# Prompt projections of q, k and the two z: three 256-column matmuls per step, or one of 512 and one of 256

## The chip, the cores and the metric

The kernel runs on one core of a Trainium2 chip. The metric is device time in microseconds of one execution: the median of three runs. One further execution was profiled; views of that profile are quoted below. Engines go by the profile's names: PE (matmul), PEld (weight load of PE), DVE, ACT, POOL (elementwise engines), SP (issues most DMAs).

## The reference

One encoder layer is applied to two inputs, a prompt of 256 tokens and a sample of 2048, each with 1024 features:

```python
def encoder_layer(x, w_in, rpb, w_fourier, b_fourier, g_pre, g_na, g_f, w_out, g_post):
    h = rms_norm(x, g_pre)
    proj = h @ w_in
    q, k, v, z_a, u_f, z_f = jnp.split(proj, ...)   # 512 columns each
    y_a = neighbourhood_attention(q, k, v, rpb)
    y_f = fourier_mix(u_f, w_fourier, b_fourier)
    mixed = jnp.concatenate([rms_norm(y_a, g_na) * jax.nn.silu(z_a),
                             rms_norm(y_f, g_f) * jax.nn.silu(z_f)], axis=-1)
    out = mixed @ w_out
    return x + rms_norm(out, g_post)
```

The change concerns four of the six projections of the prompt: z_f, z_a, k and q, with silu taken of the two z at once.

## The kernel before

Everything is float32. A product is made of three matmuls in the rounded type fp32r: each operand is split into a high part (a rounded copy, made by ACT) and a low part (the operand less its high part, made by DVE), and high x high, low x high and high x low are added up in PSUM. `mm3` issues these three (lines 164 to 166).

The kernel first projects v and u of the prompt and of part of the sample (to 72 us in the profile). Then comes the loop that is changed: 16 blocks, `for b in range(16)`, with `kind, blk = divmod(b, 4)`: blocks 0 to 3 are z_f, 4 to 7 z_a, 8 to 11 k, 12 to 15 q. A block holds 128 output features for all 256 prompt tokens; it sums over 8 steps k of 128 input features. Weights are the stationary side; the tokens (`ph`, `pl` in the profile, made once ahead of the loop from `xp`) are the moving side, 256 columns. So a block is 8 x 3 matmuls of 256 columns into one PSUM tile `mm`. PSUM tiles `mm` rotate over five buffers. After block b, ACT empties it into a tile `f` (three buffers) with Silu for blocks 0 to 7 and as a plain copy for 8 to 15 (line 806); for z_f and k the copy also reorders the tokens. SP stores `f` to memory (lines 808 and 810).

Other work is written out between the blocks, in program order on each engine:

- `wz_load` in blocks 1 to 9: SP loads raw weights `wr`, four or more blocks before they are split.
- `b_raw(b + 2)` in blocks 2 to 13: ACT makes `wh` (below: wh(b + 2)), DVE makes `wl` (wl(b + 2)), lines 575 to 579. So the weights of a block are split two blocks ahead of it.
- `n_scale` in blocks 2 to 7: two DVE scalings of sample tokens, `nx` (line 413).
- `n_sum` in blocks 8 to 11: one DVE sum or difference of 2048 elements each (line 436).
- `n_first` in blocks 5, 12 and 14: ACT makes `xh`, DVE `xl` of sample tokens (lines 441 and 442).
- `op_split` in blocks 14 and 15: ACT and DVE make `vh` and `vl`, the first two of the weights that the next stage uses (lines 490 and 491).

The next stage, `vu`, projects sample tokens in groups of 12 matmuls of 512 columns; its groups j = 0, 1, 2 ... come two at a time and use the split weights `vh`, `vl` of number j. The weights for j = 2 and 3 are loaded by SP (line 476) behind the store of block 15. ACT empties the groups of j = 0 (line 521).

Nothing runs on POOL during the loop. In later stages it subtracts and adds elementwise, among them 128x512 sums of raw weights (line 545) beside DVE's splits of weights (line 560).

Of the kernel before, what the change touches and what calls it, by code (L numbers as in the profile page):

```python
# [11 lines left out]
F32R = mybir.dt.float32r  # L12
AF = mybir.ActivationFunctionType
ALU = mybir.AluOpType
# [3 lines left out]
TP, TS = 256, 2048  # L18
T = TP + TS
D = 1024  # L20
KC = 8
# [141 lines left out]
def mm3(nc, out, lh, ll, rh, rl, first, last):  # L163
    nc.tensor.matmul(out, lh, rh, start=first, stop=False)  # L164
    nc.tensor.matmul(out, lh, rl, start=False, stop=False)  # L165
    nc.tensor.matmul(out, ll, rh, start=False, stop=last)  # L166
# [8 lines left out]
def build(tc, A, O):  # L175
    nc = tc.nc
# [48 lines left out]
    def mmt(n):  # L225
        x = mmc[0] % 5 > 2
        mmc[0] += 1
        return ps.tile([128, n], F32, tag="t" if x else "a", name="mm", bufs=2 if x else 3)
# [24 lines left out]
    def k8(dtype, name, shape=(128, 4, 512)):  # L253
        return hp.tile(list(shape), dtype, tag="k8", name=name, bufs=NK)
# [35 lines left out]
    def x_split(c, ks=slice(0, 8), vec=False):  # L290
        if c not in xh:
            xh[c] = gt(BS, F32R, "xh"), gt(BS, F32R, "xl")
        h, l = xh[c][0][:, ks], xh[c][1][:, ks]
        src = x_first(c, ks.start // 2) if c < 3 else xs[c][:, ks]
        (nc.vector.tensor_copy if vec else nc.scalar.copy)(h, src)
        nc.vector.tensor_tensor(out=l, in0=src, in1=h.bitcast(F32), op=ALU.subtract)
# [24 lines left out]
    def iv_rows(c0, n):  # L321
        ivr[c0] = ps.tile([128, 128], F32, tag="c", name="ivt", bufs=1)[:n]
        nc.tensor.transpose(ivr[c0], invt[:, c0:c0 + n], ident)
# [6 lines left out]
    def iv_get(c0, n):  # L330
        t = ivb[c0] = st.tile([128, 512], F32, tag="e", name="iv", bufs=6) if n == 2 else \
            hp.tile([128, 1024], F32, tag="vw", name="iv", bufs=3)
        nc.sync.dma_start(t[:, :128 * n],
                          ivD[c0:c0 + n].rearrange("(o c) p -> o (c p)", o=1).to_broadcast([128, 128 * n]))

    def p_mm(m, c, kps, kks=None):
        if (m, c) not in acc:
            acc[m, c] = ps.tile([128, 512], F32, tag="b", name="mm", bufs=2) if (m, c) == ("u", 2) else mmt(512)
        xh_, xl_ = xh[c]
        for kk in kks or range(2 * kps[0], 2 * kps[-1] + 2):  # L340
            (mm3 if kk > 1 or m == "u" else mm3x)(nc, acc[m, c], xh_[:, kk], xl_[:, kk], W[m][kk][0], W[m][kk][1],
                                                  kk == 0, kk == KC - 1)

    def vu_out(m, c):
        s, b = PL[c]
        o = st.tile([128, 512], F32, tag="f", name=m + "o", bufs=3)
        x = row_tile(c)
        nc.scalar.activation(o, acc.pop((m, c)), AF.Copy, scale=invt[:, x:x + 1])
        if s is not None:
            put_rows(m, 0, b, s, o)  # L350
        elif m == "u":
            nc.sync.dma_start(uD[c * 128:c * 128 + 128, :], o)
        else:
            for r in range(4):
                nc.sync.dma_start(vP[c, r, 8 * c:8 * c + 32], o[32 * r:32 * r + 32])
                x = 24 * (1 - c)
                nc.sync.dma_start(vP[1 - c, r, 32 * c:32 * c + 8], o[32 * r + x:32 * r + x + 8])
# [38 lines left out]
    f_ = lambda t: t.bitcast(F32)  # L396

    def n_load(x):
        if type(x) is tuple:
            nq[x] = k8(F32, "nx")  # L400
            nc.sync.dma_start(nq[x], A["xq"][0, x[0], x[1]])
            return
        nx = [k8(F32, "nx") for kh in range(2)]
        for kh in range(2):
            for b in range(2):
                nq[x, kh, b] = nx[kh][:, 2 * b:2 * b + 2]
                nc.sync.dma_start(nq[x, kh, b], A["xq"][1, kh, b][:, 2 * x:2 * x + 2])
# [57 lines left out]
    def r_put(x):  # L465
        nc.sync.dma_start(sD[x], (RU[1], RV[0], RU[0], RU[1], RV[1])[x])
# [26 lines left out]
    def et(name):  # L493
        return st.tile([128, 512], F32, tag="e", name=name, bufs=6)
# [76 lines left out]
    def b_raw(b):  # L571
        wh, wl = [gt(BS, F32R, "w" + x) for x in "hl"]
        src = wp_[b]
        if b < 12:
            nc.scalar.copy(wh, src)
            nc.vector.tensor_tensor(out=wl, in0=src, in1=wh.bitcast(F32), op=ALU.subtract)
        else:
            nc.scalar.activation(wh, src, AF.Copy, scale=-0.125)
            nc.vector.scalar_tensor_tensor(out=wl, in0=src, scalar=-0.125, in1=wh.bitcast(F32), op0=ALU.mult,
                                           op1=ALU.subtract)  # L580
        wb[b] = wh, wl
# [46 lines left out]
    def x_first(c, kp):  # L628
        return x0[kp][:, 8 * (kp == 0):][:, :768].rearrange("p (c k t) -> p c k t", c=3, t=128)[:, c]
# [79 lines left out]
    def wz_load(n):  # L709
        for x in range(n):  # L710
            wp_.append(load(BS, A["wz"][len(wp_)], "wr"))
# [17 lines left out]
    for c in range(3, 6):  # L729
        if c == 3:  # L730
            iv_get(0, 2)
        if c < 5:
            wz_load(3)
            x_split(c + 1)
        if c == 3:
            r_put(1)
        if c == 4:
            n_load((0, 0))
            iv_get(2, 8)
            r_put(2)  # L740
            xp = k8(F32, "xp", (128, KC, 256))
            hp_, lp_ = [k8(F32R, "p" + x, (128, KC, 256)) for x in "hl"]
            for k in range(KC):
                for t in range(2):
                    ts = slice(128 * t, 128 * t + 128)
                    nc.vector.scalar_tensor_tensor(out=xp[:, k, ts], in0=x_first(t, k // 2)[:, k % 2], scalar=gpre[:, k:k + 1],
                                                   in1=ivb[0][:, ts], op0=ALU.mult, op1=ALU.mult)
            nc.scalar.copy(hp_, xp)
            nc.vector.tensor_tensor(out=lp_, in0=xp, in1=f_(hp_), op=ALU.subtract)
        if c == 5:  # L750
            n_load((1, 0))
            b_raw(0)
            b_raw(1)
        p_mm("v", c, range(4))
        vu_out("v", c)
        if c == 5:
            b_raw(2)
            b_raw(3)
            wz_load(1)
            n_load((0, 1))  # L760
            n_scale(None, 0, 0)
            n_first(0)
        p_mm("u", c, range(4))
        if c == 3:
            iv_rows(2, 8)
        vu_out("u", c)
        if c == 3:
            iv_put(2, 8)


    for b in range(16):
        kind, blk = divmod(b, 4)
        if 1 <= b < 10:
            wz_load(1)
        if b == 2:
            n_load((1, 1))
        if b in (5, 7):
            r_put(b // 2 + 1)
        if b == 10:
            op_load(0)  # L780
        if b == 12:
            op_load(1)
        if 2 <= b < 14:
            b_raw(b + 2)
        if 2 <= b < 8:
            x, y = divmod(b, 2)
            n_scale(None, *divmod(x, 2)[::-1], range(2 * y, 2 * y + 2))
        elif 8 <= b < 12:
            n_sum(b - 8)
        if b in (5, 12):  # L790
            n_first((5, 12).index(b) + 1)
        if b > 13:
            op_split(b - 14)
        if b == 14:
            n_first(3)
        p = mmt(512)[:, :TP]
        wh, wl = wb.pop(b)
        for k in range(KC):
            mm3(nc, p, wh[:, k], wl[:, k], hp_[:, k], lp_[:, k], k == 0, k == KC - 1)
        o = st.tile([128, 256], F32, tag="f", name="f", bufs=3)  # L800
        if kind % 2:
            i, d = p, o
        else:
            i = p.rearrange("p (b r c) -> p b r c", b=2, c=32)
            d = o.rearrange("p (r b c) -> p b r c", b=2, c=32)
        nc.scalar.activation(d, i, AF.Silu if kind < 2 else AF.Copy)
        if kind < 2:
            nc.sync.dma_start(zD[kind, blk * 128:blk * 128 + 128, :TP], o)
        else:
            nc.sync.dma_start((kD if kind == 2 else qD)[blk, :, :TP], o)  # L810
# [42 lines left out]
    for i in range(16):  # L853
# [14 lines left out]
        kind, blk = divmod(2 * pair(i), 4)  # L868
        o = [st.tile([128, 1024], F32, tag="f", name="f", bufs=3) for x in range(2)]
# [31 lines left out]
        for j in range(7):  # L901
            for f, d in ((u_load, 0), (u_split, 4), (u_stage1, 6)):
                x = 7 * pr + j - 7 - d
# [33 lines left out]
            if sg == 0:  # L937
                x, y = divmod(7 * (pr - 1) + j, 14)
# [29 lines left out]
            p = mmt(512)  # L968
# [673 lines left out]
    for k in range(2, len(G) + 1):  # L1642
        pr, i = divmod(k, 9)
# [17 lines left out]
        if k in WK:  # L1661
            y = WK.index(k)
            nc.sync.dma_start(WO[y % 2][:, y // 2].bitcast(F32), woD[y % 2, y // 2])
        x = k // 2 + 1
# [65 lines left out]
        if 32 <= k < 36:  # L1730
            x, d = k - 32, atiles[k - 32]
# [120 lines left out]
```

## Time and profile before

| what | us |
|---|---|
| median of 3 runs (lowest to highest) | 958.73 (958.66 to 958.79) |
| span of the profiled execution, first to last instruction | 957.4 |
| PE busy in it | 949.5 |
| DVE, ACT, POOL busy in it | 707.8, 494.8, 435.4 |
| the 16 blocks, first matmul to the next stage's first | 72.00 to 118.28 |

For the profiled execution no time besides its span is given; the span lies 1.3 us below the median of the runs. In the rows of the profile a line holds start and duration in us, or a count, a total and a mean; "x2" at a row's end says that two instructions were merged, and their joint stretch is given. Instructions on one engine start up to 0.1 us before the row ahead of them ends, since an engine takes up the next while it finishes the last. A matmul's duration includes its way through the array; the distance between two starts is what it costs. "out<-in" are the program's names for tiles.

### The profile page before, as it was taken

How to read it: one execution, taken by the hardware profiler on the slowest of the kernel's cores; microseconds unless marked ns; L12 is line 12 of the kernel's file. 1: busy time of each engine (PE TensorE's matmuls, PEld its weight loads, DVE VectorE, ACT ScalarE, POOL GpSimd, SP SyncE). 2: the span in 40 equal slices, each digit the busy share in tenths (PEclk: the TensorE clock that was granted, in tenths of full speed). 3: DMA queues.
4: the chain of work that ended last, by engine and by line, in shares of the span. 5: the costliest groups of instructions: out<-in, count | busy, mean ns of one | idle time of the engine just before them, and what ended most of it. 6: DMA issues, size and time to landing. Idle time of an engine off the chain costs nothing.

```text
span 957.4 us, 16751 instructions
## 1 busy us (share of the span) xinstructions
PE 949.5 (99%) x5625; PEld 790.3 (83%) x5625; DVE 707.8 (74%) x1298; ACT 494.8 (52%) x1068; POOL 435.4 (45%) x411
## 2 busy tenths in 40 slices
PE   9999999999999999999999999999999999999997
PEld 8889988888888888888888779788788888888886
DVE  6758987787975865697887369776666656659997
ACT  6735676423334532233344267677676766644443
POOL 4100002465750302575566055567678686524444
PEclk9999999999999999999999999999999999999998
DMA  9899697557758894499889997788877998989993
GB/s 357 297 383 334 245 343 264 187 193 280 296 190 331 304 342 144 175 345 356 306 297 340 335 329 247 232 241 271 262 241 239 285 301 255 287 289 346 330 346 129
DMA packets 140077, 269.80 MB, mean 282 GB/s; under 512 B 13178, under 2 KB 80464, under 8 KB 136728
## 3 DMA queue, kind: packets, MB, share of 16 engines
q1 hardware_dynamic: 139640, 268.32, 80.5%
q8 instruction: 45, 0.74, 0.3%
q10 hardware_dynamic: 288, 0.40, 0.1%
q14 instruction: 40, 0.33, 0.1%
q0 software_dynamic: 64, 0.02, 0.0%
HBM read 179.00 MB, written 96.81 MB: 288 GB/s over the span
## 4 chain that ended last, share of the span: by engine, by line
PE 98%; DVE 1%; DMA 0%; issue 0%; DVEq 0%
PE po L1497 20%; PE mm L166 18%; PE mm L164 18%; PE mm L165 18%; PE pv L1586 6%; PE ptb L1570 6%; PE s L1229 4%; PE py L164 1%; PE py L165 1%; PE py L166 1%; PE ptb L1043 1%; DMA x<-x 0%; PE pab L1053 0%; PE ppq L1096 0%; PE pz L166 0%; PE pz L164 0%
## 5 line engine op out<-in xcount | busy, mean ns | idle before, releaser
L164 PE MATMUL mm<-xh,wa 128*128 128x512 f32 x448 | 174.4, 389 | 0.0
L165 PE MATMUL mm<-xl,wa 128*128 128x512 f32 x448 | 174.3, 389 | 0.0
L166 PE MATMUL mm<-xh,wa 128*128 128x512 f32 x448 | 174.3, 389 | 0.0
L545 POOL TENSOR_TENSOR ws<-wr 128x512 f32<-128x512 f32 x16 | 23.4, 1465 | 217.8 <-DVE wa L560 127.6
L1263 POOL TENSOR_SCALAR w<-w,m 128x465 f32<-128x465 f32 (+9 forms) x136 | 84.8, 635 | 46.2 <-DVE m L1260 35.5
L166 PEld LDWEIGHTS mm<-xh,wa 128*128 128x128 f32 x448 | 84.1, 188 | 17.6
L164 PEld LDWEIGHTS mm<-xh,wa 128*128 128x128 f32 x448 | 84.1, 188 | 17.5
L165 PEld LDWEIGHTS mm<-xl,wa 128*128 128x128 f32 x448 | 84.1, 188 | 17.4
L1497 PE MATMUL po<-wo,yh 128*128 128x512 f32 x272 | 90.5, 414 | 0.0
L560 DVE TENSOR_TENSOR wa<-wr,wa 128x512 fp32r<-128x512 f32 x60 | 71.8, 1205 | 22.0 <-ACT wa L559 21.8
L1497 PE MATMUL po<-w,yh 128*128 128x512 f32 x280 | 86.8, 391 | 0.0
L1256 ACT ACTIVATE w<-w,m 128x465 f32<-128x465 f32 (+9 forms) x136 | 78.3, 579 | 13.7 <-DVE m L1251 13.3
L1251 DVE CUSTOM_DVE_ANT_1 w<-s,tb 128x465 f32<-128x465 f32 (+8 forms) x124 | 61.2, 531 | 10.1 <-PE s L1229 9.6
L165 PE MATMUL mm<-vl,xh 128*128 128x512 f32 x168 | 65.5, 390 | 0.0
L598 POOL TENSOR_TENSOR mt<-mt,rmask 128x880 f32<-128x880 f32 (+2 forms) x24 | 50.8, 2129 | 32.2 <-DVE mt L594 20.1
L164 PE MATMUL mm<-vh,xh 128*128 128x512 f32 x168 | 65.4, 389 | 0.0
L166 PE MATMUL mm<-vh,xl 128*128 128x512 f32 x168 | 65.4, 389 | 0.0
L1574 DVE COPY pt<-ptb 120x384 f32<-120x384 f32 (+5 forms) x72 | 40.5, 562 | 28.6 <-PE ptb L1570 27.8
L891 DVE TENSOR_TENSOR f<-u,mm 128x512 f32<-128x512 f32 x64 | 43.4, 679 | 24.2 <-PE mm L166 19.7
L1497 PEld LDWEIGHTS po<-w,yh 128*128 128x128 f32 x280 | 52.2, 188 | 10.9 <-issue 0.4
L1570 PE MATMUL ptb<-ident,w 128*120 128x128 f32 (+8 forms) x422 | 58.8, 276 | 0.0
L1586 PEld LDWEIGHTS pv<-pt,v 120*64 120x64 f32 (+9 forms) x880 | 47.4, 136 | 12.9 <-issue 9.7
(287 smaller groups left out, 2369.8 us busy)
## 6 DMA issues: line engine op xcount, KB each, us to landing
wr<-wz SPq DMA_DIRECT2D x48, 512.0 KB
vl<-sD SPq DMA_DIRECT2D x20, 512.0 KB
xm<-xm SPq DMA_DIRECT2D x9, 1024.0 KB
oD<-ofs SPq DMA_DIRECT2D x18, 512.0 KB
of<-oD SPq DMA_DIRECT2D x18, 512.0 KB
yr<-yD SPq DMA_DIRECT2D x34, 256.0 KB
zD<-f SPq DMA_DIRECT2D x16, 512.0 KB
xD<-nx SPq DMA_DIRECT2D x14, 512.0 KB
```

Source lines behind the costliest of these rows:

```text
L164: nc.tensor.matmul(out, lh, rh, start=first, stop=False)
L165: nc.tensor.matmul(out, lh, rl, start=False, stop=False)
L166: nc.tensor.matmul(out, ll, rh, start=False, stop=last)
L560: nc.vector.tensor_tensor(out=o[:, 1], in0=src, in1=o[:, 0].bitcast(F32), op=ALU.subtract)
L598: nc.gpsimd.tensor_tensor(out=o, in0=i, in1=rmask[:, m0:m0 + n].unsqueeze(2).to_broadcast([128, n, 80]), op=ALU.add)
L891: nc.vector.tensor_tensor(out=dst(f, b), in0=src(uu[u]), in1=src(p), op=op)
L1251: nc.vector.tensor_tensor_reduce(out=rows(g["w"][b][:, h, :n], w), in0=rows(g["s"][2 * b + h][:, :nr * sw(w)], sw(w))[:, :, :w], in1=tv, s ...
L1256: nc.scalar.activation(w, w, AF.Exp, bias=m[:, h:h + 1], scale=-1.0, accum_out=m[:, 2 + h:3 + h])
L1263: nc.gpsimd.tensor_scalar(w, w, m[:, 4 + h:5 + h], 1.0, ALU.mult, ALU.mult)
L1497: nc.tensor.matmul(p, (d["l"] if x == 2 else d["h"])[:, c], w(n, int(x == 1), c), start=j == 0, stop=j == 11)
L1570: nc.tensor.transpose(ptb[h][:nk, j * 128:j * 128 + 128], g["w"][b][:, h, c0:c0 + nk], ident)
L1586: nc.tensor.matmul(p[hs, b], g["v"][:nk, v, hs], g["pt"][b][:nk, h, j * 128:j * 128 + 128], start=j == 0, stop=j == len(ch) - 1)
```

## The change

The high and the low part of the tokens are laid side by side: `pp` is two tiles (for k 0 to 3 and 4 to 7) in which each k has 256 columns of high and then 256 of low. Each step k then takes two matmuls: the weights' high part times all 512 columns, and the weights' low part times the 256 high columns, which adds into the left half of the same PSUM tile. The tile ends with two halves that have to be added.

```diff
-            hp_, lp_ = [k8(F32R, "p" + x, (128, KC, 256)) for x in "hl"]
+            pp = [k8(F32R, "p%d" % x, (128, 4, 2, 256)) for x in range(2)]
...
-            nc.scalar.copy(hp_, xp)
-            nc.vector.tensor_tensor(out=lp_, in0=xp, in1=f_(hp_), op=ALU.subtract)
+            for x in range(2):
+                src, (h, l) = xp[:, 4 * x:4 * x + 4], [pp[x][:, :, y] for y in range(2)]
+                nc.scalar.copy(h, src)
+                nc.vector.tensor_tensor(out=l, in0=src, in1=f_(h), op=ALU.subtract)
...
-        p = mmt(512)[:, :TP]
+        p = mmt(512)
         wh, wl = wb.pop(b)
         for k in range(KC):
-            mm3(nc, p, wh[:, k], wl[:, k], hp_[:, k], lp_[:, k], k == 0, k == KC - 1)
+            x = pp[k // 4][:, k % 4]
+            nc.tensor.matmul(p, wh[:, k], x.rearrange("p y t -> p (y t)"), start=k == 0, stop=k == KC - 1)
+            nc.tensor.matmul(p[:, :TP], wl[:, k], x[:, 0], start=False, stop=k == KC - 1, skip_group_check=True)
         o = st.tile([128, 256], F32, tag="f", name="f", bufs=3)
-        if kind % 2:
-            i, d = p, o
-        else:
-            i = p.rearrange("p (b r c) -> p b r c", b=2, c=32)
+        t = et("t")
+        nc.scalar.copy(t, p)
+        i, j, d = t[:, :TP], t[:, TP:], o
+        if kind % 2 == 0:
+            i, j = [x.rearrange("p (b r c) -> p b r c", b=2, c=32) for x in (i, j)]
             d = o.rearrange("p (r b c) -> p b r c", b=2, c=32)
-        nc.scalar.activation(d, i, AF.Silu if kind < 2 else AF.Copy)
+        nc.gpsimd.tensor_tensor(out=d, in0=i, in1=j, op=ALU.add)
+        if kind < 2:
+            nc.scalar.activation(o, o, AF.Silu)
```

The emptying of a block thus becomes: ACT copies 512 columns to a tile `t` (below: copy t(b)), POOL adds its halves into `f` (add(b)), and for blocks 0 to 7 ACT takes Silu of `f` in place (Silu(b)). Stores and all other work keep their places in the program.

On PE, one step k of block 0 stood like this before, where `ph` and `pl` are the tokens' parts and `wh`, `wl` the weights':

```order
L164 MATMUL mm<-ph,wh 128x256
L165 MATMUL mm<-pl,wh 128x256
L166 MATMUL mm<-ph,wl 128x256
L164 MATMUL mm<-ph,wh 128x256
L165 MATMUL mm<-pl,wh 128x256
L166 MATMUL mm<-ph,wl 128x256
```

Two steps are shown. The same two steps after the change, with `p_587` the first of the two tiles `pp`:

```order
L802 MATMUL mm<-p_587,wh 128x512
L803 MATMUL mm<-p_587,wl 128x256
L802 MATMUL mm<-p_587,wh 128x512
L803 MATMUL mm<-p_587,wl 128x256
```

The use of `wl` moves from the third place of a step to the second.

On ACT, from the cast of wh(7) to the drain of block 8, before:

```order
L575 CAST wh<-wr 128x1024
L441 CAST xh<-nx 128x2048
L806 ACTIVATE f<-mm 128x256
L575 CAST wh<-wr 128x1024
L806 ACTIVATE f<-mm 128x256
L575 CAST wh<-wr 128x1024
L806 ACTIVATE f<-mm 128x256
L575 CAST wh<-wr 128x1024
L806 ACTIVATE f<-mm 128x2x4x32
```

And the same stretch after:

```order
L575 CAST wh<-wr 128x1024
L441 CAST xh<-nx 128x2048
L806 COPY t<-mm 128x512
L813 ACTIVATE f<-f 128x256
L575 CAST wh<-wr 128x1024
L806 COPY t<-mm 128x512
L813 ACTIVATE f<-f 128x256
L575 CAST wh<-wr 128x1024
L806 COPY t<-mm 128x512
L813 ACTIVATE f<-f 128x256
L575 CAST wh<-wr 128x1024
L806 COPY t<-mm 128x512
```

Each cast of weights now stands behind a Silu that reads what POOL wrote.

On POOL, the difference at the loop, between the prompt's folding of u (`ru`) and the sums of raw weights (`ws`) of a later stage:

```order
 L278 TENSOR_TENSOR ru<-wr 128x2x8x31 x8
+L811 TENSOR_TENSOR f<-t 128x2x4x32 x4
+L811 TENSOR_TENSOR f<-t 128x256 x4
+L811 TENSOR_TENSOR f<-t 128x2x4x32 x4
+L811 TENSOR_TENSOR f<-t 128x256 x4
 L545 TENSOR_TENSOR ws<-wr 128x512
```

Sixteen adds are new on an engine that had nothing in this stretch.

## The prediction

> **What bounds the kernel now.** I read the page's busy shares and chain first, then the three stretches around the changed loop, then rows of single instructions.
>
> ```profile
> span 957.4 us, 16751 instructions
> PE 949.5 (99%) x5625; PEld 790.3 (83%) x5625; DVE 707.8 (74%) x1298; ACT 494.8 (52%) x1068; POOL 435.4 (45%) x411
> PE 98%; DVE 1%; DMA 0%; issue 0%; DVEq 0%
> 77.90:87.90 10.00, 10.00 (x86) 10.00 (x85) 7.65 (x9) 5.21 (x9) 0.00 (x0) 1.00 0.90 333
> 87.90:124.40 36.50, 36.50 (x280) 35.30 (x280) 36.40 (x27) 23.43 (x30) 0.00 (x0) 1.00 0.78 273
> 124.40:160.00 35.60, 35.60 (x158) 29.47 (x157) 29.27 (x32) 24.90 (x34) 5.92 (x4) 1.00 0.85 312
> ```
>
> The stretches' columns are length, then busy time (count) of PE, PEld, DVE, ACT and POOL, the granted clock, DMA share and GB/s. Over the whole run PE is the end of every chain, so a microsecond that PE loses anywhere is a microsecond of the result. The changed loop (72 to 118 us) is unlike the average: from 87.9 to 124.4 DVE is busy 36.40 of 36.50 us, and POOL does nothing. So in the loop's second half PE and DVE are both full, and the question is which ends last. These rows show it:
>
> ```profile
> 72.00 0.28 PE L164 MATMUL mm<-ph,wh 128*128 128x256 f32 x1
> 115.20 0.28 PE L164 MATMUL mm<-ph,wh 128*128 128x256 f32 x1
> 115.32 0.28 PE L165 MATMUL mm<-pl,wh 128*128 128x256 f32 x1
> 115.55 0.39 PE L166 MATMUL mm<-ph,wl 128*128 128x256 f32 x1
> 118.28 0.40 PE L164 MATMUL mm<-vh,xh 128*128 128x512 f32 x1
> 114.28 1.21 DVE L579 SCALAR_TENSOR_TENSOR wl<-wr,wh 128x1024 fp32r<-128x1024 f32 x1
> PEld mm L166 <- DVE wl L579: 0.2, 1, 0.2
> ```
>
> Block 0 starts at 72.00 and block 15 at 115.20: 43.2 us for 15 blocks of 24 matmuls, 120 ns each, 2.88 us a block. In block 15 the third matmul should start at 115.44 and starts at 115.55, because wl(15) is only ready at 115.49 (114.28 + 1.21). That is the waits' 0.2 us row. So DVE already decides block 15's end; a faster PE gets past it only if DVE's chain ends sooner.
>
> **The change part by part.** *Matmuls.* Per k, three 256-column matmuls become one of 512 and one of 256.
>
> ```profile
> 121.71 0.39 PE L164 MATMUL mm<-vh,xh 128*128 128x512 f32 x1
> 122.84 0.39 PE L166 MATMUL mm<-vh,xl 128*128 128x512 f32 x1
> ```
>
> These are five matmuls apart: 226 to 227 ns for 512 columns. Twice 120 is 240, so pairing two saves 13 ns: 128 times, 1.7 us. A block is then 8 x (0.227 + 0.120) = 2.78 us. The Trainium skill, TensorE: Matmul & The Clock Gate, section Back-to-back issue gap, gives 262 cycles for 256 columns and 518 for 512 at 2.4 GHz; by that a pairing would save 2.5 ns and the loop 0.3 us. The rows' 13 ns is used. Either way it is below 0.2% of the time (1.9 us), which is about what a measurement of this kernel can tell from no change.
>
> *Drain.* One 0.38 us ACT instruction per block becomes an ACT copy of 512 columns, a POOL add of 256, and for blocks 0 to 7 a second ACT instruction (Silu) that waits for the add. What these cost:
>
> ```profile
> 123.95 0.59 ACT L521 COPY uc<-mm 128x512 f32<-128x512 f32 x1 [2.13 <-PE mm L166]
> L1209 POOL TENSOR_TENSOR ql<-ql,qh x36: 725/735/744, 575.5 to 837.9; 128x256 fp32r<-128x256 f32 x36
> L560 DVE TENSOR_TENSOR wa<-ws,wa x24: 677/1186/2304, 155.5 to 518.5; 128x512 fp32r<-128x512 f32 x24
> 154.80 1.29 POOL L545 TENSOR_TENSOR wr<-wr 128x512 f32<-128x512 f32 x1
> 156.05 1.74 POOL L545 TENSOR_TENSOR wr<-wr,ws 128x512 f32<-128x512 f32 x1
> 155.53 1.11 DVE L560 TENSOR_TENSOR wa<-ws,wa 128x512 fp32r<-128x512 f32 x1 [2.41 <-ACT wa L559]
> 155.53 2.81 DVE L560 TENSOR_TENSOR wa<-ws,wa 128x512 fp32r<-128x512 f32 x2 [2.41 <-ACT wa L559]
> ```
>
> The copy is 0.59, the add 0.735 alone, the Silu about the old 0.38. But POOL and DVE take turns. The DVE subtraction at 155.53 needs 0.68 alone; it ends at 156.64, 0.55 after POOL's 154.80 instruction ends (156.09). POOL's next, issued at 156.05, needs 1.29 alone and ends at 157.79, 1.15 after DVE's end. DVE's second (the pair ends at 158.34) again ends 0.55 after POOL. Nothing overlaps but about 0.14 of start-up. All DVE work in the loop (weights' low parts, scalings, sums) is of this form: two SBUF inputs. A 256-column add therefore takes 0.735 - 0.14 = 0.59 between two DVE instructions, and as DVE's own start-up hides too, sets DVE back by about 0.55. Bounds: 0, if adds fell into idle DVE time, and 0.73, with no overlap. DVE has 0.1 us idle in 36.5, so I take 0.55. The Trainium skill, SBUF — State Buffer, section SBUF: two separate sides, calls this an exclusive lock, held for a whole instruction; the rows above agree.
>
> *ACT's cycle, blocks 2 to 7.* ACT's order is now: cast wh(b+2), copy t(b), Silu(b), cast wh(b+3).
>
> ```profile
> 75.46 0.68 ACT L348 ACTIVATE uo<-mm,invt 128x512 f32<-128x512 f32 x1
> 76.15 1.28 ACT L806 ACT_TABLE_LOAD   x1
> 78.29 1.04 ACT L575 CAST wh<-wr 128x1024 fp32r<-128x1024 f32 x1
> 81.17 1.04 ACT L575 CAST wh<-wr 128x1024 fp32r<-128x1024 f32 x1
> 75.59 2.29 DVE L442 TENSOR_TENSOR xl<-nx,xh 128x2048 fp32r<-128x2048 f32 x1 [1.98 <-ACT xh L441]
> 82.24 1.22 DVE L576 TENSOR_TENSOR wl<-wr,wh 128x1024 fp32r<-128x1024 f32 x1 [0.33 <-ACT wh L575]
> 87.86 1.91 ACT L441 CAST xh<-nx 128x2048 fp32r<-128x2048 f32 x1
> 90.47 2.29 DVE L442 TENSOR_TENSOR xl<-nx,xh 128x2048 fp32r<-128x2048 f32 x1
> 92.67 1.22 DVE L576 TENSOR_TENSOR wl<-wr,wh 128x1024 fp32r<-128x1024 f32 x1
> 93.81 1.41 DVE L413 SCALAR_TENSOR_TENSOR nx<-nx,gpre,iv 128x512 f32<-128x512 f32 x2
> ```
>
> A cast takes 1.04 and starts DVE's wl at once (81.17, then 82.24). The copy follows the cast (0.59), so the add asks for its turn while wl runs 1.22, and ends 0.59 after it; Silu starts 0.1 later, the next cast 0.28 after that (the gap seen between an ACT drain and the cast behind it). Cycle: 1.07 + 1.22 + 0.59 + 0.1 + 0.28 = 3.25 us, against PE's 2.78 and 2.88 before. The start is late too: copy t(0) at 76.1, add(0) behind DVE's 2.29 of 75.59 until 78.5 (the table load hides there), Silu(0), copy t(1), add(1), Silu(1), so the cast of wh(4) starts at 80.6, not 78.29. Then wh(5) 83.85, wh(6) 87.1, wh(7) 90.3. DVE's wl(7) ends at 90.3 + 1.07 + 1.22 = 92.6; behind it on DVE come two scalings (1.3), add(5) (0.6), xl of the next stage's tokens (2.2), add(6) (0.6) and wl(8) (1.14): 98.4. Before, wl(8) ended at 92.67 + 1.22 = 93.89. It is **4.5 us late**, and PE, which would want it at 94.4, stalls about 4 us by then.
>
> *DVE's chain, blocks 8 to 15.* From wl(8) to wl(15) DVE ran without a gap before, 93.89 to 115.49. The same work now has add(7) to add(13) between: 7 x 0.55 = **3.9 us**. wl(15) ends at 115.49 + 4.5 + 3.9 = 123.9. Block 15's first use of it is now its second matmul, so the loop ends 0.07 - 0.23 + 2.78 = 2.6 later, at 126.5. The next stage began at 118.28: **+8.2 us**. The matmuls' 1.7 us are gone in the waits.
>
> *After the loop.* Adds 14 and 15 put DVE 1.1 later still, and xl (2.28) goes ahead of add(15):
>
> ```profile
> 119.89 2.35 DVE L491 TENSOR_TENSOR vl<-vr,vh 128x1024 fp32r<-128x1024 f32 x2
> 119.52 1.82 SPq L476 DMA_DIRECT2D vl<-sD  x4
> 124.43 2.00 ACT L490 CAST vh<-vl 128x1024 fp32r<-128x1024 f32 x2
> 118.70 0.38 ACT L806 ACTIVATE f<-mm 128x256 f32<-128x256 f32 x1
> ```
>
> PE's group j=1 starts 24 matmuls after 118.28, at 123.7, and its vl was ready at 122.24: 1.5 us to spare for 1.3 lost, so it is covered, barely. The four vl loads queue on SP behind q's last store, which waits for add(15) (about 129.4, against 119.1 for the old drain): they issue 10.4 later while PE is 8.2 later. In the old run they had landed for the cast at 124.43; shifted, the cast ends by about 136 and its subtraction by 137.2, where PE wants the first at 118.28 + 8.2 + 48 x 0.227 = 137.4. Covered; 1 us of stall is the upper end.
>
> *At nothing:* the tokens' split in two halves ends about 62 us, ten before block 0 needs it. Stores and the weight loads behind them on SP move with their drains, and a load is issued four blocks (11 us) ahead of its use. PSUM: five buffers rotate, and t(b) lags PE by up to 4 us, not four blocks.
>
> The sum against the profiled span: 957.4 + 8.2 = 965.6. The runs' median, 958.73, lies 1.3 above that span, so I forecast 958.7 + 8.1 = **966.8 us**.
>
> **The rivals.** *The turns cost little, so no change.* If adds slipped beside DVE (its price 0), ACT's cycle would be 0.95 + 0.48 + 0.1 + 0.73 + 0.1 + 0.28 = 2.64, under PE's 2.78. DVE's chain would then end wl(15) between 115.5 (cast of wh(8) in time) and 117.1 (wh(4) still 1.6 late through the Silu's wait). The loop ends between 118.1 and 119.7, so 958.5 to 960.1. It decides this if DVE's instructions in the loop keep their 1.22 and 2.28 us. Against it: the L560 row's maximum of 2304 ns beside a minimum of 677. A gain over 1.9 us is not to be had even so, since the matmuls save 1.7.
>
> *Only one of the two losses.* If PE's stalls let ACT catch up, or POOL's request finds the gaps that they open, either the 4.5 or the 3.9 us stays: 960.5 to 964.5. For it: a stalled PE also delays t(b), which moves adds. Against it: DVE, not PE, is the full engine from block 8, and it has no gaps.
>
> *More.* Adds at 0.73 each on 9 occasions add 1.6, the late vl loads 1: 968.5 to 970.
>
> **How the numbers follow.** As summed (963.5 to 969.5): 0.68. Only part of the loss (960.6 to 963.5): 0.13. Turns cost little (956 to 960.6): 0.15. More than 969.5: 0.04. The range of 8 in 10 runs from 962.0 to 969.5. Slower by over 0.2%: 0.85; within: 0.12; faster: 0.03, the end of the third case below 956.8, were 512-column matmuls cheaper beside 256-column ones than in the row.
>
> **What would show it.** Right: L802 and L803 matmuls 0.227 and 0.120 apart inside a block; L811 adds of 0.73 to 2.9 us; DVE's wl up to 1.8 instead of 1.22; PE idle about 3 us in front of block 8, then about 1.1 us a block, put down to DVE wl; the next stage starting near 126.5. Wrong: wl still 1.22 under an add; blocks back to back 2.78 us apart; a stage start near 118; or PE stalls at j=1 and j=2 behind vl.

## The result, and the profile after

The changed kernel takes **968.66 us** (median of four executions, 967.57 to 969.99), the kernel before 958.76 in the same job (958.66 to 959.35). The ratio is 1.0103, 95% interval 1.0089 to 1.0116: about 1% slower, 1.9 us above the forecast and inside its range. The profiled execution is the longest of the four; its own time is 969.99 us, its span 968.2. All positions below are microseconds of the profiled span.

The page's head of the changed kernel, then the same three stretches (length, busy time and count of PE, PEld, DVE, ACT and POOL, granted clock, DMA share, GB/s), with their ends moved along with the loop's:

```profile
span 968.2 us, 16549 instructions
PE 952.7 (98%) x5497; PEld 784.1 (81%) x5497; DVE 714.9 (74%) x1299; ACT 502.1 (52%) x1077; POOL 453.7 (47%) x427
...
PE 84%; DVE 3%; issue 2%; DMA 1%; ACT 0%; POOL 0%; DVEq 0%; ACTq 0%
...
77.90:87.90 10.00, 10.00 (x59) 8.68 (x58) 6.04 (x6) 6.29 (x10) 4.53 (x4) 1.00 0.66 216
87.90:132.40 44.50, 37.80 (x196) 30.30 (x196) 44.08 (x31) 29.58 (x36) 15.01 (x13) 1.00 0.68 231
132.40:170.00 37.60, 37.11 (x163) 29.91 (x162) 31.66 (x31) 24.60 (x32) 6.22 (x4) 1.00 0.88 322
```

In the loop's second half DVE is as full as before (44.08 of 44.50 us), but PE no longer is (37.80). PE's share of the last chain falls from 98% to 84%, and DVE and DMA come into it. Where the 10.8 us of span went is read from four matmuls of the timeline (start, duration, engine, line, operation):

```profile
73.72 0.39 PE L802 MATMUL mm<-p,wh 128*128 128x512 f32 x1
...
100.10 0.39 PE L803 MATMUL mm<-p,wl 128*128 128x256 f32 x1 [1.92 <-DVE wl L576]
...
128.21 0.40 PE L164 MATMUL mm<-vh,xh 128*128 128x512 f32 x1
...
167.50 0.39 PE L164 MATMUL mm<-xh,wa 128*128 128x512 f32 x1
```

| part | before | after | change | forecast |
|---|---|---|---|---|
| ahead of block 0 | 72.00 | 73.72 | +1.7 | 0 |
| the 16 blocks | 46.28 | 54.49 | **+8.2** | **+8.2** |
| next stage, up to the first matmul on `wa` | 38.11 | 39.29 | +1.2 | 0, at most 1 |
| all after it | 801.0 | 800.7 | -0.3 | 0 |

Inside the loop: ACT's casts, a DVE instruction under a POOL add and the last `wl`, POOL's longest add, and two sums of waits (engine, line, what was waited for: total us, times, longest):

```profile
82.29 1.03 ACT L575 CAST wh<-wr 128x1024 fp32r<-128x1024 f32 x1
...
85.54 1.03 ACT L575 CAST wh<-wr 128x1024 fp32r<-128x1024 f32 x1
...
88.78 1.04 ACT L575 CAST wh<-wr 128x1024 fp32r<-128x1024 f32 x1
...
98.31 1.74 DVE L576 TENSOR_TENSOR wl<-wr,wh 128x1024 fp32r<-128x1024 f32 x1
...
119.83 1.76 DVE L579 SCALAR_TENSOR_TENSOR wl<-wr,wh 128x1024 fp32r<-128x1024 f32 x1
121.51 2.82 DVE L442 TENSOR_TENSOR xl<-nx,xh 128x2048 fp32r<-128x2048 f32 x1
124.25 1.21 DVE L579 SCALAR_TENSOR_TENSOR wl<-wr,wh 128x1024 fp32r<-128x1024 f32 x1
...
106.67 2.19 POOL L811 TENSOR_TENSOR f<-t 128x256 f32<-128x256 f32 x1 [1.69 <-ACT t L806]
...
PEld mm L803 <- DVE wl L576: 4.8, 6, 2.2
...
PEld mm L803 <- DVE wl L579: 4.5, 4, 1.1
```

ACT's cycle is 3.25 us, as forecast. Where an add takes its turn, DVE's `wl` lasts 1.76 instead of 1.21 and `xl` 2.82 instead of 2.28: 0.54 each. PE waits for `wl` in blocks 6 to 15, 2.2 us in block 8 and about 1 us each from block 11 on.

The 1.7 us ahead of the loop lie in the first 12 us of the profile, where nothing was changed. These are two stretches with PE's busy time and count, granted clock, DMA share and GB/s, of the kernel before:

```profile
4.00:12.00 8.00, 7.95 (x33) 1.00 1.03 400
12.00:72.00 60.00, 60.00 (x267) 1.00 0.91 352
```

and of the changed kernel:

```profile
4.00:12.00 8.00, 7.51 (x26) 1.00 1.03 408
12.00:72.00 60.00, 60.00 (x267) 1.00 0.93 353
```

26 matmuls against 33 at the start, and 267 in both afterwards. In the changed kernel the first matmul on `wc` begins at 6.12 instead of 5.68, and from 6.71 on eight starts in a row are 0.43 us apart, where the kernel before is at 0.23 from 7.08 on; the clock column shows nothing of it. In the ten profiles of the experiments below, whose programs are the changed kernel's up to the loop, block 0 starts at 71.6 to 72.05 us. So this is a late start of that one execution, not the change; without it the span would be 966.5.

### The profile page after: what moved, and what is told of

Same layout as the page of the kernel before. It is cut to its first block, busy times and chain, and to the rows that moved or that the text cites. A ratio compares the mean times of both kernels' runs of the same rounds, so it can differ in the third digit from the quotient of the medians.

```text
span 968.2 us, 16549 instructions
## 1 busy us (share of the span) xinstructions
PE 952.7 (98%) x5497; PEld 784.1 (81%) x5497; DVE 714.9 (74%) x1299; ACT 502.1 (52%) x1077; POOL 453.7 (47%) x427
## 4 chain that ended last, share of the span: by engine, by line
PE 84%; DVE 3%; issue 2%; DMA 1%; ACT 0%; POOL 0%; DVEq 0%; ACTq 0%
PE po L1504 20%; PE mm L165 14%; PE mm L166 14%; PE mm L164 14%; PE pv L1593 6%; PE ptb L1577 6%; PE s L1236 4%; PE py L164 1%; PE py L165 1%; PE py L166 1%; PE ptb L1050 1%; DMA vl<-sD 1%; DVE nx L436 1%; DVE xl L442 1%; DVE vl L491 0%
## 5 line engine op out<-in xcount | busy, mean ns | idle before, releaser
L811 POOL TENSOR_TENSOR f<-t 128x256 f32<-128x256 f32 x16 | 19.5, 1221 | 84.0 <-DMA nx<-xq 50.9
```

## The experiments

The theory is the prediction's: POOL's add takes turns out of DVE's full chain, and makes ACT's cycle longer than PE's block. The rivals are that the matmuls or the longer chain of waits cost the time, and that POOL's adds are slipped in for little. Times are medians; ratios are against the kernel before in the same job, with their 95% intervals. "Loop" is the first matmul of block 0 to the next stage's first, "next stage" from there to the first matmul on `wa`.

**Only the pairs of matmuls.**

```
  p = mmt(512); per k: one 512-column matmul (wh x high|low), one of 256 (wl x high)
- copy to t, POOL add, Silu
+ nc.scalar.activation(d, p[:, :TP], Silu or Copy)    # as before
```

> Only the matmuls are changed: 512 and 256 columns per step as in the changed kernel, but a block is emptied as before, by one ACT instruction from the left 256 columns. The product of the weights' high and the tokens' low part is left out of the result. Theory (DVE's chain of split weights decides the loop's second half, the drain makes the loss): a block takes 2.78 us instead of 2.88 until DVE's chain catches it; wl(15) ends 0 to 0.5 us sooner, the loop lasts 45.6 to 46.1 us instead of 46.28, so 0.2 to 0.6 us less than before (958.1 to 958.5). Rival 1, PE alone bounds the loop: 1.7 us less, 957.0, with no stall in blocks 13 to 15. Rival 2, the 512-column matmuls beside 256-column ones make the loss: about 8 us more, 967.

Measured: 958.48 us, ratio 0.9995 (0.9986 to 1.0004); loop 45.96 us. Rows of PE and DVE at the end of its loop:

```profile
114.05 1.22 DVE L579 SCALAR_TENSOR_TENSOR wl<-wr,wh 128x1024 fp32r<-128x1024 f32 x1
...
114.67 0.40 PE L802 MATMUL mm<-p,wh 128*128 128x512 f32 x1
...
115.32 0.39 PE L803 MATMUL mm<-p,wl 128*128 128x256 f32 x1 [0.25 <-DVE wl L579]
115.54 0.39 PE L802 MATMUL mm<-p,wh 128*128 128x512 f32 x1
```

PE's blocks are 2.82 us apart instead of 2.88, and block 15 then waits for wl(15), ready at 115.27 (115.49 before). The matmuls cost nothing and bring nothing that can be measured: this is the upper end of what the change could have brought, with a merge that costs nothing. DVE's chain sets the end even without the new drain.

**Only the new drain.**

```
- nc.tensor.matmul(p, wh[:, k], x.rearrange("p y t -> p (y t)"), ...)
+ nc.tensor.matmul(p[:, :TP], wh[:, k], x[:, 0], ...)
+ nc.tensor.matmul(p[:, TP:], wh[:, k], x[:, 1], ...)
```

> Only the drain is changed: three matmuls of 256 columns a step as before, but the high x low one goes into the right half of the PSUM tile, and the block is emptied by ACT copy, POOL add and Silu as in the changed kernel. Theory (the drain makes the loss): the loop lasts 54.2 to 54.8 us, as in the changed kernel (54.5), and the time is that of the changed kernel within 1 us, 967 to 970. Rival, the pairing makes the loss: near 959. Mixed, the pairing still saves PE time that counts: 1.7 us over the changed kernel, 970.4.

Measured: 967.84 us, ratio 1.0089 (1.0074 to 1.0105); loop 54.54, next stage 39.04. The whole loss is there without a single pair. Part of its sums is missing (the first output is off by about a third), but it issues as many matmuls as the kernel before, so its time can be read. In the loop the two one-part kernels together account for the changed one: -0.3 and +8.3 us against +8.2. In the time they come to -0.4 and +9.0 against +9.9.

**POOL writes, but reads nothing.**

```
- nc.gpsimd.tensor_tensor(out=d, in0=i, in1=j, op=ALU.add)
+ nc.gpsimd.memset(t, 0.0)
```

> The changed kernel, but where POOL added the halves it writes zeros over all 512 columns of t, reading nothing; ACT's Silu (blocks 0 to 7) or the store (8 to 15) takes the left half of t after that. The sums are left out of the result. The chain ACT, POOL, ACT stays; a POOL write of 512 columns on 32 partitions took 0.51 us in the profile. Theory (POOL and DVE take turns because both read SBUF through one port): DVE's wl keeps 1.22 us in every block, ACT's cycle is 2.4 us, under PE's 2.78, and the loop lasts 46.5 to 47.5 us; time 959.0 to 960.5. Rival 1, turns are taken for any POOL instruction: wl up to 1.75 us as in the changed kernel, loop 52 to 53, time 965 to 967. Rival 2, the detour of ACT over POOL makes the loss whatever POOL does: loop 50 or more.

Measured: 959.60 us, ratio 1.0007 (0.9998 to 1.0016); loop 47.16, next stage 38.11. POOL's and DVE's rows:

```profile
106.61 0.53 POOL L807 MEMSET t<- 128x512 f32 x1 [2.30 <-ACT t L806]
...
105.99 2.29 DVE L436 TENSOR_TENSOR nx<-nt,nx 128x2048 f32<-128x2048 f32 x1
...
110.82 0.53 POOL L807 MEMSET t<- 128x512 f32 x1 [3.68 <-ACT t L806]
...
109.33 2.29 DVE L436 TENSOR_TENSOR nx<-nx 128x2048 f32<-128x2048 f32 x1
...
111.53 1.23 DVE L579 SCALAR_TENSOR_TENSOR wl<-wr,wh 128x1024 fp32r<-128x1024 f32 x1
```

Both memsets run in the middle of a DVE instruction (105.99 and 109.33), and neither side is lengthened. The order of waits ACT, POOL, ACT is still there, so of the 8.2 us about 7.3 (54.49 less 47.16) belong to the turns that POOL's add takes; the other 0.9 is left to the longer chain of waits. The Trainium skill, SBUF — State Buffer, section SBUF: two separate sides, limits the lock, for a DVE instruction with two SBUF inputs, to a GpSimd instruction that reads SBUF; these rows agree. The memset is also shorter than the add (0.53 against 0.73 us) and of another kind, so that it is the reading that takes the turn rests on this one pair of kernels and is not shown beyond it.

**Each add of k and q twice.**

```
  nc.gpsimd.tensor_tensor(out=d, in0=i, in1=j, op=ALU.add)
+ if kind > 1:
+     nc.gpsimd.tensor_tensor(out=d, in0=i, in1=j, op=ALU.add)
```

> The changed kernel, with POOL's add of blocks 8 to 15 (k and q) issued twice into the same buffer; the result is the same. Theory (each POOL add that reads SBUF takes a turn of 0.55 us out of DVE's full chain): seven further turns lie between wl(8) and wl(15), 3.9 us; the loop takes 57 to 58.5 us instead of 54.5, and the time is 971 to 973 us. In between, if part of the second adds falls into DVE's remaining waits: 970 us. Rival (DVE's chain is not what ends last, or POOL is simply held off by it): the loop stays at 54 to 55 us and the time at 967 to 969 us.

Measured: 975.18 us (median of four executions, of which one took 2435 us and is left out of the ratio), ratio 1.0161 (1.0144 to 1.0178); loop 56.61, next stage 43.63. DVE and POOL:

```profile
117.56 2.66 POOL L813 TENSOR_TENSOR f<-t 128x256 f32<-128x256 f32 x1
...
119.55 1.75 DVE L579 SCALAR_TENSOR_TENSOR wl<-wr,wh 128x1024 fp32r<-128x1024 f32 x1
...
120.17 1.72 POOL L811 TENSOR_TENSOR f<-t 128x256 f32<-128x256 f32 x1
...
121.22 2.82 DVE L442 TENSOR_TENSOR xl<-nx,xh 128x2048 fp32r<-128x2048 f32 x1
```

Now every DVE instruction of the stretch is lengthened. Starts of blocks 12 to 15 are 4.42 us apart, against 3.88 in the changed kernel and 3.34 for the same DVE instructions without adds (wl(14) to wl(15) before: 110.94 to 114.28). Steps of 0.54 per turn, twice. The loop grew less than expected, because five second adds, not seven, lie ahead of wl(15): block 8's own add comes only at 103. The time grew more, because SP's loads for the next stage stand behind the later stores: that stage lost 4.3 us more. PE waited there for 3.7 us in all, and its next ten matmuls cost another 1.6, at a granted clock of 0.68 (142.07 to 147.40).

**Silu one block later.** ACT then no longer stands waiting for the add.

```
  nc.gpsimd.tensor_tensor(out=d, in0=i, in1=j, op=ALU.add)
- Silu(b) and store(b) here
+ if late: late.pop()()        # Silu(b-1) and its store, ahead of block b's add
```

> The changed kernel, but Silu(b) and its store stand one block later on ACT, behind copy t(b+1), so that ACT does not wait for POOL between the copy and the next cast. All adds stay. Theory (two losses of about equal size: ACT's cycle through POOL in blocks 0 to 7, and POOL's turns in DVE's chain): wl(8) is 2 us late instead of 4.4, wl(15) 5.9 instead of 8.1; the loop lasts 52.0 us instead of 54.5, the time is about 966.2, 2.4 us under the changed kernel. Rival, the turns alone make the loss: unchanged, 968 to 969. Rival, ACT's wait alone makes it: loop near 46, time near 959.5.

Measured: **972.20 us**, ratio 1.0139 (1.0126 to 1.0153); loop 57.74, next stage 41.79. A miss: 6 us slower than expected. POOL's, SP's, ACT's, DVE's and PE's rows:

```profile
101.30 18.35 POOL L814 TENSOR_TENSOR f<-t 128x256 f32<-128x256 f32 x3 [3.97 <-ACT t L807]
...
115.40 2.28 DVE L442 TENSOR_TENSOR xl<-nx,xh 128x2048 fp32r<-128x2048 f32 x1
...
118.31 0.32 SPq L821 DMA_DIRECT2D kD<-f  x1
118.72 0.38 SPq L244 DMA_DIRECT2D wr<-wz  x1
...
122.80 1.06 ACT L578 ACTIVATE wh<-wr 128x1024 fp32r<-128x1024 f32 x1 [9.29 <-DMA wr<-wz]
...
123.89 1.22 DVE L579 SCALAR_TENSOR_TENSOR wl<-wr,wh 128x1024 fp32r<-128x1024 f32 x1 [6.21 <-ACT wh L578]
...
PE mm L803 <- ACT wh L578: 5.5, 1, 5.5
```

Three adds are merged in the first row. The first is block 8's: issued at 101.30, it lasted 16.99, to 118.29, 0.6 after the last of nine further DVE instructions that ran without a gap (115.40 + 2.28 = 117.68). POOL was not given a turn at all, and DVE's instructions kept their 1.22 and 2.28. That should have been the best case; but the store of block 8 waited for the add, and behind it on SP waited the load of the last block's raw weights. Issued at 118.72, it held up wh(15), wl(15) and PE. The theory missed before that, too: wl(8) was ready 24.89 us after block 0's start (95.53 + 1.21, less 71.85), 3.0 late where 2.0 was expected. So ACT's wait made only 1.4 of the 4.4 us; wl(4) still starts 1.8 late, and each pair of scalings behind a split lasts 1.89 instead of 1.41.

**The same, with the stores out of the way.**

```
+ if len(kept) > 2: store(b - 2)     # k and q: two blocks later
  if b == 10: op_load(0)
+             op_load(1)             # was at b == 12
```

> The kernel with Silu one block later, and on SP the stores of k and q two blocks later, and the load of the next stage's second group two blocks earlier, so that no load stands behind a store that waits for an add. Theory (the 9.3 us wait of that kernel's last cast was SP's queue, not DVE): even where POOL is held off, DVE's chain goes on to block 15; the loop takes 46 to 50 us, the time is 958.5 to 963 us. Rival (POOL gets its turns now as in the changed kernel, since nothing fixes who gets the port): DVE's chain has 3.9 us of turns but not the 4.5 us of ACT's cycle, the loop takes 50 to 52.5 us, the time is 962.5 to 966 us. Second rival (the held-off adds block ACT through the buffers of t, or the late stores block the next stage): 968 us and more.

Measured: 969.09 us, ratio 1.0103 (1.0070 to 1.0137); the profiled execution, at 965.21 us, has a loop of 52.96 and a next stage of 38.12. The loads no longer wait: SP's order was the cause of the 9.3 us. But the loop is no better than the first rival's 50 to 52.5. Stretches around block 8, and rows of POOL and DVE:

```profile
97.00:100.80 3.80, 3.80 (x14) 0.55 0.99 410
...
101.68 10.82 POOL L813 TENSOR_TENSOR f<-t 128x256 f32<-128x256 f32 x3 [4.55 <-ACT t L806]
...
105.20 2.28 DVE L436 TENSOR_TENSOR nx<-nx 128x2048 f32<-128x2048 f32 x1
...
107.64 1.52 DVE L579 SCALAR_TENSOR_TENSOR wl<-wr,wh 128x1024 fp32r<-128x1024 f32 x1 [0.16 <-ACT wh L578]
...
111.83 1.76 DVE L579 SCALAR_TENSOR_TENSOR wl<-wr,wh 128x1024 fp32r<-128x1024 f32 x1
```

POOL was held off from 101.68 until DVE paused for 0.16 us at 107.48 to wait for ACT; from then on the turns came back, and blocks 13 to 15 took 4.2, 3.9 and 4.4 us: 4.0 us more than three blocks of 2.82. Block 8 took 6.57: 2.1 us of waiting for wl(8), which the adds of the earlier blocks had made late, and 1.6 us because the granted clock then fell to 0.55. Those two sums, 4.0 and 3.7, are the distance from 45.2 (16 blocks of 2.825) to 53, but for 0.1.

Its four executions lay between 965.2 and 972.0 us, so it ran again, unchanged:

> The kernel silu_late_stores_late once more, unchanged: its four executions lay between 965.2 and 972.0 us, and only one of them left a trace. Theory (whether POOL gets a turn or is held off is decided anew in each execution): this trace shows another pattern of long adds on POOL than 6.4 us for the first, and the times spread by some us again; a longer hold-off goes with a longer time, because stores and loads stand behind the held add. Rival (the pattern is fixed by the program): the same 6.4 us hold-off of block 8's add and a loop of 53.0 us, to 0.2 us, whatever the time.

Measured: 966.27 us (966.22 to 971.78, four executions); loop 52.98, next stage 38.97. The first add was held off from 101.80, again for 6.39 us, and the blocks are as above to 0.1 us. So two traces show one pattern, and the theory of a new draw in each execution is not borne out. The executions near 972 us left no trace; what they did differently stays open.

**Loads ahead of the last store.** On the changed kernel itself:

```
+ if b == 15:
+     op_load(2); op_load(3)     # ahead of q's last store, not behind it
```

> The changed kernel, with the four loads of low parts for the next stage's groups 2 and 3 issued on SP ahead of the last store of q instead of behind it. Theory (the loads come late because SP waits for the last add): the next stage's time up to the first matmul on wa falls from 39.3 to 38.1 us, the loop stays at 54.5, the time is 966.5 to 967.8 us. Rival (the loads collide with other transfers and nothing is gained): 39.3 us stay, and so does the time, 968 to 969 us.

Measured: 966.91 us, ratio 1.0083 (1.0068 to 1.0098); loop 54.47, next stage 38.12. As expected, the 1.2 us after the loop are gone. In the changed kernel their rows were these (ACT's wait for DMA, and the two matmuls that came late, by about 0.5 us each with the one behind):

```profile
ACT vh L490 <- DMA vl<-sD: 3.2, 2, 1.8
...
141.13 0.50 PE L165 MATMUL mm<-vl,xh 128*128 128x512 f32 x1 [0.27 <-DVE vl L491]
...
145.74 0.50 PE L165 MATMUL mm<-vl,xh 128*128 128x512 f32 x1 [0.23 <-DVE vl L491]
```

**The merge on DVE.**

```
- nc.scalar.copy(t, p)
+ nc.scalar.copy(t[:, TP:], p[:, TP:])
- nc.gpsimd.tensor_tensor(out=d, in0=t[:, :TP], in1=t[:, TP:], op=ALU.add)
+ nc.vector.tensor_tensor(out=d, in0=p[:, :TP], in1=t[:, TP:], op=ALU.add)   # ahead of wl(b+3); Silu a block later
```

> The changed kernel with the merge on DVE: ACT copies only the right half out of PSUM (256 columns), DVE adds the left half in PSUM to it ahead of the next block's wl, and the Silu comes one block later. The result is that of the changed kernel, and POOL does nothing in the loop. A DVE addition of 512 columns with one PSUM input takes 0.68 us and starts 0.60 behind the one before, so 256 columns are estimated at 0.3 to 0.4. Theory (DVE's chain sets the end): seven to fourteen of them on that chain, 2.5 to 5 us; the loop takes 48.5 to 51 us, the time is 961 to 963.5 us. Rival (DVE now waits for PE's blocks and PE for DVE's, so that the waits add up): the loop takes 54 us or more, the time is 967 us or more.

Measured: 965.06 us, ratio 1.0067 (1.0050 to 1.0084); loop 50.19, next stage 39.99. DVE:

```profile
114.16 0.42 DVE L818 TENSOR_TENSOR f<-mm,t 128x256 f32<-128x256 f32 x1
114.50 1.21 DVE L579 SCALAR_TENSOR_TENSOR wl<-wr,wh 128x1024 fp32r<-128x1024 f32 x1
115.63 2.28 DVE L442 TENSOR_TENSOR xl<-nx,xh 128x2048 fp32r<-128x2048 f32 x1
117.83 0.42 DVE L818 TENSOR_TENSOR f<-mm,t 128x256 f32<-128x256 f32 x1
```

An add costs 0.34 from start to start, and blocks 12 to 15 are 3.67 apart: 3.34 plus one add. The loop came out as expected, the time 1.6 us above, since the next stage's loads were late here too.

> Both working edits together: the merge on DVE (half a copy on ACT, DVE's addition with one PSUM input, Silu one block later), and the next stage's four loads on SP ahead of the last store of q. The result is that of the changed kernel. Theory (the two losses add up and are independent): the loop stays at 50.2 us, since DVE's chain is 0.33 us longer in every block, and the time up to the first matmul on wa falls from 40.0 to 38.1 us; the time is 962.8 to 963.5 us, still 4 us behind the kernel before. Rival (the late loads were the price of DVE's additions after the loop, not of SP's order): 40 us stay, and the time is 964.5 to 965.5 us.

Measured: 963.13 us, ratio 1.0045 (1.0030 to 1.0060); loop 50.19, next stage 38.10. The two edits add up. It is the best version that leaves nothing out, 5.5 us ahead of the changed kernel and 4.4 behind the kernel before. With `pairs_alone` at 0.9995, which leaves the merge out, no version here beats the kernel before.

## Why the prediction was right, and where its sizes were off

- **ACT's cycle and wl(8).** Right. The cycle is 3.25 us, and wl(8) is ready at 100.05 (98.31 + 1.74), 26.33 after block 0's start against 21.89 before: 4.4 us late, 4.5 forecast. `silu_one_block_later` shows that ACT's wait for the add is only 1.4 of it.
- **Turns on DVE's chain.** Right. wl(15) is ready at 125.46, 51.74 after block 0's start against 43.49: 8.25 late, so 3.8 us between wl(8) and wl(15), for seven turns of 0.54. `drain_alone`, `pool_only_writes` and `adds_twice` show that the turns are the cause, not the drain's longer chain of waits. What the prediction did not see is that this alternation is no law: with another order POOL got no turn for 17 us.
- **Matmuls.** The saving was mis-sized, without effect. A pair with its 256-column matmul is 353 ns, not 347: 235 for the 512 columns between narrower matmuls, where the row with 512 on both sides gave 227. So a pairing saves 7 ns and the loop 0.9 us, not 1.7. An estimate from the figures of the Trainium skill, TensorE: Matmul & The Clock Gate, section Back-to-back issue gap, gives 0.3; the runs lie between. The waits swallowed all of it, as forecast.
- **After the loop.** This step failed: "covered" was 1.2 us of stall, a little over its upper end of 1 us. For group j = 2 the first half of `vl` came in time, as summed: ready at 138.59 (137.36 + 1.23), wanted at 139.35. What the prediction left out is the second half, which waited for its own load: ready at 141.07 (139.85 + 1.22), it held PE up by about 0.5 us, and the first half for j = 3 did so again. So a sign that it gave for being wrong, a stall of PE at j = 2 behind `vl`, was seen. The reason was the one it named, the loads behind the store that waits for the last add, as `loads_ahead_of_store` shows.
- **The sum.** 965.6 us of span was forecast. Without the late start the profiled span is 966.5, and 0.9 of the difference is that stall with the 0.3 gained later. The other three executions have spans of 965.8 to 967.1. The time was 1.9 us above the forecast, and about 0.5 of that is the step from span to time: in each of the four executions the time is 1.8 us above its own span, where the prediction took 1.3 from a span and a median of different executions. The late start of 1.7 us is in no step, and no step could have held it.
- **The rivals.** "The turns cost little" is what `pool_only_writes` did, at 959.6 us, inside that rival's 958.5 to 960.1: the right time for a POOL instruction that takes no turn. "Only one of the two losses" came nowhere near.

## What to carry to other kernels

Before work is given to an idle engine, ask which engine it will take turns with and whether that one is full: here an add of 0.73 us on an idle POOL cost the full DVE 0.54, and the same add on DVE itself 0.34. The saving on PE was worth nothing in a stretch that another engine's chain ended, so read that stretch's last wait first. And look at what stands behind a store on its queue: a store that waits makes loads late that have nothing to do with it.

## What was not expected of the hardware

- POOL can be held off for long: 17 us behind nine DVE instructions without a gap in `silu_one_block_later`, 6.4 us twice in `silu_late_stores_late`, until DVE paused. In the changed kernel and in `adds_twice`, with the same kinds of instructions in the same order and no gap, POOL got its turn after the DVE instruction that was running. What decides it stays open. The Trainium skill, SBUF — State Buffer, section SBUF: two separate sides, has whichever starts first take the pair for its instruction, and the other blocked meanwhile; that covers the turns, and does not say why a waiting add is passed over nine times.
- A stall of PE can cost more than its length: after 2.1 us without a matmul in block 8 of `silu_late_stores_late`, the granted clock was 0.55 over the next 3.8 us. In the changed kernel a stall of the same length at the same place was followed by none of this. In `loads_ahead_of_store`, whose program is the same up to block 15's matmuls, it was. The rows of the two, in this order:

```profile
99.50:103.00 3.50, 2.90 (x16) 1.00 0.85 242
...
99.50:103.00 3.50, 3.50 (x13) 0.52 0.85 281
```

  So the program of the loop does not decide it. There it cost nothing (loop 54.47 against 54.49), since DVE's chain ended the loop.

  The Trainium skill, TensorE: Matmul & The Clock Gate, section Part 1: The HAM clock gate, speaks of free-running windows of about 3.4 us; a stall that only sometimes lowers the clock fits that, but no run here shows the windows.
